# A decoder layer on one core: single rows' maxima, sums and a copy moved behind the prompt's join and copy, memory keys turned behind shares, roots written in place

## The chip, the cores and the metric

The kernel runs on one core of one Trainium2 chip. The metric is the device time of one execution in microseconds (us), lower is better. The core's engines run side by side, each through its own list of instructions in order: TensorE (PE, with PEld for its weight loads), VectorE (DVE), ScalarE (ACT), GpSimd (POOL) and SyncE (SP), which issues most transfers. Semaphores tie the lists together.

## What is computed

One layer of a hybrid decoder for a prompt of 512 rows and a sample group of 8 sequences of 4 rows, with the same weights (model width 1024, float32). Each sub-layer is normalised before and after (RMS norm) and added to the residual:

```python
# 1. mixer: one input projection, split into mLSTM heads and differential-attention heads
p = softmax(mask(q @ k.T) * 64 ** -0.5)       # two components a head, 4 heads
a = p[:, :, 0] - lam * p[:, :, 1]             # the "join"
o = a @ v                                     # then a norm of each head, a gain, w_out
# sample rows: the same, over 256 cached keys read through a page table, and 4 new ones
# 2. memory attention: q = w_mq(norm(x)), 4 heads of 256 over 256 memory tokens,
#    prompt: keys and values from mem_prompt; sample: cache_mem_k, cache_mem_v of each sequence
# 3. ConvFFN: up projection, causal depthwise conv of width 3, SiLU gate, down projection
def rms_norm(x, g):
    return x * lax.rsqrt(jnp.mean(x * x, axis=-1, keepdims=True) + 1e-6) * g
```

## The kernel before

Rows are tiled by 128: four prompt tiles and one of 32 sample rows. Projections run at full precision from two parts of a number each: a weight stage `wst` of 512 KB is loaded by SP, ACT casts its high part (L146) and DVE subtracts to get the low part (L147), together a slot `wslot`. The pool of slots holds four; `Weights` keeps a plan of slots and emits the next as one comes free (`plan`, `pump`, `free`); a slot in the set `extra` comes from another pool, called through `S`, and is emitted without taking one of the four. TensorE then does three matmuls a block: high by high (L411), high by low (L412) and low by high (L413), or the like in L472 and L485.

The order of instructions on each engine is set by a scheduler that goes through the program in the order in which it is written, with a model of each engine's time; `tc.issue_after(x)` holds the instructions written under it until after x. The differential attention goes in steps of one prompt tile and head, sixteen in all, through a software pipe: `da_soft` (two score products `sda`, negated maxima `nm` L1260 on DVE, two exponentials `pda` with sums `su` L1261 on ACT, the reciprocal L1263, L1264 and the join `pda` L1265 on DVE), two turns later `da_turn` (transposes `tpa` L1273 on PE, copied to `aT` L1275 on ACT), then `da_av` (`oda` L1285) and, after every fourth step, `da_end`, which calls `da_post` (square `dasq` L1099 on ACT, sums `dass` L1101 on DVE, root `dars` L304 and product L1103 on POOL, transposes `dat` L1106 on PE, `dtm` L1108 on DVE).

Between the prompt's steps go those of the sample's sequences, in pairs: keys `tpk` are turned on PE (L1229) and copied to `kT` (L1230, one half of them on ACT, one on DVE), scores `ssc` (L1242), a mask added on DVE (L1245), then `sample_exp` (negated maximum `snm` L1052 on DVE, exponential `das` L1053 on ACT). When all eight are done, `sample_softmax` weighs them into one block (`spa` L1072), copies that on ACT to `spc` (L1074), takes two prompt steps (`between`, which is `step` at the call), and turns the copy (`spt` L1085).

In the memory attention `ch_soft` is a prompt step (scores `sca` L1455, maxima `cnm` L1459, exponentials `cp` L1462, reciprocal `csu` L1463, shares `cp` L1465 on DVE) and `ch_turn` turns the shares on PE (`cpt` L1474) and splits them to `pT`; `ch_out` multiplies by the values (`cpo` L1486). Each sequence's keys are 1024 wide in two tiles; `mk_turn` turns one sequence's on DVE by two block transposes of 128x1024 in place (`kvt` or `wst`, L1508), `mk_scores` makes `ssc` (L1528). `ql` (L1439) is the low part of the queries, made on DVE from `w_mq`'s product.

`rstd` writes the root of a mean square into a small tile `rs` on POOL (L302, L304). After it a copy on DVE put it where it is used: in `mrs` at the start (L540, twice) and in `rsd` (L1178, five times, at each projection's end that is followed by a norm); `rsd` is spread over partitions by PE (`rsb` L1737), and the normalised rows are turned (`tp` L332), scaled to `ht` (L334) and split into `fT` (L146 on ACT, L147 on POOL). The last prompt tile's end (L1953 to L1956) adds the residual in three pieces, columns 0 to 511 and 768 to 1023 on DVE and 512 to 767 on POOL, and stores each from SP.

Of the kernel before, what the change touches and what calls it, by code (L numbers as in the profile page):

```python
# [12 lines left out]
ALU = mybir.AluOpType  # L13
# [64 lines left out]
def kernel(ctx: ExitStack, tc: tile.TileContext, I, O):  # L78
# [145 lines left out]

    def slotA(w, k0, n0, nrow=256, share=False):
        def emit():
            st, s = v2(stage(), 512), slot_tile()
            sv = s.rearrange("p l (k n) -> p l k n", k=2)
# [11 lines left out]

    def slotsA(w, n0, share=False):
        for k in range(0, 8, 2):
            slotA(w, k, n0, share=share)

# [52 lines left out]

    def rstd(ss, n, w, dim, name="rs"):

        r = small(w, name)  # L300
        if dim is not None:
            nc.gpsimd.tensor_scalar(out=r[:n], in0=ss, scalar1=1.0 / dim, scalar2=EPS, op0=MUL, op1=ADD)  # L302
            ss = r[:n]
        GTT(out=r[:n], in0=ss, in1=mhalf[:n, :w], op=ALU.pow)  # L304
        return r[:n]

# [232 lines left out]
    for b in range(2):  # L539
        VCP(out=mrs[:, b:b + 1], in_=rstd(sumsq(xms[b], P, N("hN")), P, 1, DM))  # L540
    W.nslots = NSLOT
# [513 lines left out]
    def sample_softmax(sall, su, coef, sel, oname, between=None):  # L1055
# [14 lines left out]
        for e in range(2):  # L1070
            for i in range(NB // 2):
                mm(pa[NS * i:NS * i + NS, :w], lhsT=csz[:, 2 * i + e, :], rhs=sall[:, 2 * i + e, :], start=(e == 0), stop=(e == 1))  # L1072
        a = Z("spc")[:, :w]
        nc.scalar.copy(out=a, in_=pa[:, :w])  # L1074
        behind = between() if between else None
        return a, attend_T(a, oname, behind)
# [19 lines left out]
    def da_post(o, n, c0):  # L1096
# [3 lines left out]
        ss = small(4, "dass")[:n]  # L1100
        VRED(out=ss, in_=sq, axis=AX.X, op=ADD)  # L1101
        rs = rstd(ss, n, 4, P, "dars")
# [16 lines left out]
    def proj_add(xt, gname, src, gname2, dst, order=None, scale=None):  # L1119
# [52 lines left out]
        def rows_of(x, n, c0):  # L1172
            if scale is None:
                pend.append((norm_rows(x, n, ACTROWS), n, gname2, target[0], c0, POOLQ))
                return
            pend.append((x, n, gname2, target[0], c0, POOLQ))
            rs = sm.tile([P, 1], F32, name="rsd", tag="rsd", bufs=5)
            VCP(out=rs[:n], in_=rstd(sumsq(x, n, Z("sqx").bitcast(BF16)[:n]), n, 1, DM))  # L1178
            scale[1].append((rs[:n], c0, n))
# [34 lines left out]

    kst, kts, pts, aTs, outs, rcs = {}, {}, {}, {}, {}, {}

# [15 lines left out]
    def dk_scores(b):  # L1232
# [11 lines left out]
        for c, ps in pair.items():  # L1244
            VTT(out=ps[:, 256:260], in0=ps[:, 256:260], in1=con("cm4"), op=ADD)  # L1245
            sample_exp(sall, c, ps, nm, su)

    def da_soft(i):
# [15 lines left out]
        VTS(out=rc[:, 1:2], in0=rc[:, 1:2], scalar1=su[:, 0:1], scalar2=nlam, op0=MUL, op1=MUL)  # L1264
        STT(out=pt[:, 0, :nk], in0=pt[:, 1, :nk], scalar=rc[:, 1:2], in1=pt[:, 0, :nk], op0=MUL, op1=ADD)  # L1265
        rcs[i] = rc

    def da_turn(i):
# [5 lines left out]
        aTs[i] = Z("aT")  # L1274
        nc.scalar.copy(out=aTs[i][:, :nk], in_=tp[:, :nk])  # L1275

# [30 lines left out]
    def step():  # L1307

        next(prompt)
        next(prompt)  # L1310
        return summed[0].ins

# [51 lines left out]
    for n0 in (0, 512):  # L1364
        slotsA(w_out, n0)
    for n0 in (0, 512):
# [77 lines left out]

    pTs, cps, scored = {}, {}, [None]

    def ch_soft(i):
# [16 lines left out]
        for j in range(2):  # L1464
            VTS(out=p[:, j, :], in0=p[:, j, :], scalar1=su[:, j:j + 1], scalar2=None, op0=MUL)  # L1465

# [165 lines left out]
    for b in range(0, NB, 2):  # L1632
# [3 lines left out]
        if b < 6:  # L1636
            if b:
                mk_turn(b + 2)
            mk_turn(b + 3)
            if b:  # L1640
# [212 lines left out]
    for gi, js in enumerate(groups):  # L1853
# [87 lines left out]
        def end(b):  # L1941
# [3 lines left out]
            if b == TORD[-1]:  # L1945
# [3 lines left out]
                for o, w in ((512, 256), (0, 512), (768, 256)):  # L1949
# [4 lines left out]
                    else:  # L1954
                        STT(out=xb[:, c], in0=z, scalar=rs, in1=xb[:, c], op0=MUL, op1=ADD)
                    dma(out=out[:, c], in_=xb[:, c])  # L1956
                return
# [105 lines left out]
```

## Time and profile before

| what | value |
| --- | --- |
| median of 3 runs | 934.09 us (933.4 to 935.85) |
| the profiled execution's own time | 933.45 us |
| its span | 931.7 us |
| TensorE's granted clock over the span | 0.996 |
| PE busy | 913.5 us (98%) |
| DVE busy | 606.5 us (65%) |
| ACT busy | 377.7 us (41%) |
| POOL busy | 223.0 us (24%) |
| HBM read and written | 112.54 MB and 16.93 MB, 139 GB/s over the span |

Busy time counts instructions with work, not waits or the issue of transfers. In a row of the timeline stand the start, the duration of the group (of several, if a count stands behind x), engine, line, operation and tiles; a bracket gives the idle time of that engine just before, and what ended it. Steps and sequences are named here by their number from zero, in the order of the program: tpa 5 is the transpose of the prompt's step 5.

### The profile page before, as it was taken

How to read it: one execution, taken by the hardware profiler on the slowest of the kernel's cores; microseconds unless marked ns; L12 is line 12 of the kernel's file. 1: busy time of each engine (PE TensorE's matmuls, PEld its weight loads, DVE VectorE, ACT ScalarE, POOL GpSimd, SP SyncE). 2: the span in 40 equal slices, each digit the busy share in tenths (PEclk: the TensorE clock that was granted, in tenths of full speed). 3: DMA queues.
4: the chain of work that ended last, by engine and by line, in shares of the span. 5: the costliest groups of instructions: out<-in, count | busy, mean ns of one | idle time of the engine just before them, and what ended most of it. 6: DMA issues, size and time to landing. Idle time of an engine off the chain costs nothing. (4 is left out here: it accounts for less than half of the span.)

```text
span 931.7 us, 17473 instructions
## 1 busy us (share of the span) xinstructions
PE 913.5 (98%) x6780; PEld 797.6 (86%) x6780; DVE 606.5 (65%) x1128; ACT 377.7 (41%) x728; POOL 223.0 (24%) x475
## 2 busy tenths in 40 slices
PE   9999999999999999999999999999999999999995
PEld 6899787879866778998877899899888998999974
DVE  5845144565888338768645878547748775776767
ACT  5745233344587437724534533322212221222232
POOL 6611000034442126581000642001001110110114
PEclk9999999999999999999999999999999999999998
DMA  9960023335780439966777631152044304412023
GB/s 284 313 192 4 1 91 139 91 102 164 237 294 19 136 107 293 300 214 236 293 244 194 200 108 53 38 168 69 27 137 137 91 4 131 122 47 91 25 94 118
DMA packets 120834, 130.59 MB, mean 140 GB/s; under 512 B 8599, under 2 KB 86264, under 8 KB 120752
## 3 DMA queue, kind: packets, MB, share of 16 engines
q1 hardware_dynamic: 114568, 125.96, 42.9%
q10 hardware_dynamic: 6184, 3.53, 1.2%
q8 instruction: 53, 0.87, 0.4%
q14 instruction: 29, 0.24, 0.1%
HBM read 112.54 MB, written 16.93 MB: 139 GB/s over the span
## 5 line engine op out<-in xcount | busy, mean ns | idle before, releaser
L485 PE MATMUL mm<-fT,wslot 128*128 128x256 f32 x1872 | 235.9, 288 | 0.0
L485 PEld LDWEIGHTS mm<-fT,wslot 128*128 128x128 f32 x1872 | 234.4, 188 | 1.8 <-issue 0.8
L146 ACT CAST wslot<-wst 128x1024 fp32r<-128x1024 f32 x125 | 130.4, 1049 | 255.0 <-issue 72.5
L147 DVE TENSOR_TENSOR wslot<-wst,wslot 128x1024 fp32r<-128x1024 f32 x125 | 154.2, 1239 | 76.1 <-ACT wslot L146 75.7
L1869 PE MATMUL mm<-wslot,act 128*128 128x512 f32 (+1 forms) x180 | 69.3, 387 | 0.0
L1872 PE MATMUL mm<-wslot,act 128*128 128x512 f32 (+1 forms) x172 | 67.1, 391 | 0.0
L1873 PE MATMUL mm<-wslot,act 128*128 128x512 f32 (+1 forms) x172 | 66.8, 392 | 0.0
L1771 POOL COPY cvo<-u 128x2 f32<-128x2 f32 x43 | 10.4, 242 | 217.4 <-DVE u L1769 217.4
L411 PE MATMUL mm<-wslot,hT 128*128 128x512 f32 x128 | 51.3, 402 | 0.0
L413 PE MATMUL mm<-wslot,hT 128*128 128x512 f32 x128 | 51.0, 399 | 0.0
L485 PE MATMUL mm<-hT,wslot 128*128 128x256 f32 (+1 forms) x384 | 50.9, 289 | 0.0
L412 PE MATMUL mm<-wslot,hT 128*128 128x512 f32 x128 | 50.8, 397 | 0.0
L1766 DVE TENSOR_TENSOR u<-mm,rsb 128x256 f32<-128x256 f32 x43 | 18.1, 424 | 48.4 <-PE mm L485 48.4
L485 PEld LDWEIGHTS mm<-hT,wslot 128*128 128x128 f32 x384 | 49.2, 188 | 0.5 <-issue 0.2
L1869 PEld LDWEIGHTS mm<-wslot,act 128*128 128x128 f32 x180 | 34.3, 191 | 8.0 <-issue 0.4
L1873 PEld LDWEIGHTS mm<-wslot,act 128*128 128x128 f32 x172 | 32.3, 188 | 6.9 <-issue 0.4
L1872 PEld LDWEIGHTS mm<-wslot,act 128*128 128x128 f32 x172 | 32.3, 188 | 6.9
L1783 ACT ACTIVATE c<-c 128x560 f32<-128x560 f32 x21 | 14.1, 672 | 57.2 <-DVE c L1777 57.1
L1777 DVE SCALAR_TENSOR_TENSOR c<-u,cvT,c 128x560 f32<-128x560 f32 x43 | 34.4, 799 | 0.9
L1776 DVE SCALAR_TENSOR_TENSOR c<-u,cvT,c 128x560 f32<-128x560 f32 x43 | 34.1, 794 | 0.2
L1884 DVE TENSOR_TENSOR yp<-mm,yp 128x512 f32<-128x512 f32 (+1 forms) x41 | 27.1, 673 | 4.5 <-PE mm L1873 4.3
L413 PEld LDWEIGHTS mm<-wslot,hT 128*128 128x128 f32 x128 | 24.1, 188 | 5.0
(497 smaller groups left out, 1857.5 us busy)
## 6 DMA issues: line engine op xcount, KB each, us to landing
wst<-in_w_up_dram SPq DMA_DIRECT2D x42, 512.0 KB
wst<-in_w_in_dram SPq DMA_DIRECT2D x28, 512.0 KB
wst<-in_w_down_dram SPq DMA_DIRECT2D x20, 512.0 KB
kvt<-in_cache_mem_k_dram SPq DMA_DIRECT2D x10, 512.0 KB
kvt<-in_cache_mem_v_dram SPq DMA_DIRECT2D x10, 512.0 KB
wst<-in_w_mk_dram SPq DMA_DIRECT2D x8, 512.0 KB
xb<-in_x_prompt_dram SPq DMA_DIRECT2D x8, 512.0 KB
wst<-in_cache_dk_dram SPq DMA_DIRECT2D x16, 256.0 KB
```

Source lines behind the costliest of these rows:

```text
L146: nc.scalar.copy(out=hi, in_=src)
L147: (eng or nc.vector).tensor_tensor(out=lo, in0=src, in1=f32(hi), op=SUB)
L411: mm(ps[b], lhsT=xt.hi(k, c0, c0 + n), rhs=s[:, 0, kk, :], start=(k == 0), stop=False)
L412: mm(ps[b], lhsT=xt.hi(k, c0, c0 + n), rhs=s[:, 1, kk, :], start=False, stop=False)
L413: return mm(ps[b], lhsT=xt.lo(k, c0, c0 + n), rhs=s[:, 0, kk, :], start=False, stop=(k == nk - 1))
L485: mm(ps[i], lhsT=s[:, l, k, :], rhs=x(k, c0, c1), start=(k == 0 and j == 0), stop=(k == 7 and j == 2))
L1776: STT(out=c, in0=u[:, 1:EXT - 1], scalar=w[1], in1=c, op0=MUL, op1=ADD)
L1777: STT(out=c, in0=u[:, 0:EXT - 2], scalar=w[0], in1=c, op0=MUL, op1=ADD)
L1869: mm(ps, lhsT=t[:, 0, c0:c0 + P], rhs=s[:, 0, i % 2, cs], start=st, stop=False)
L1872: mm(ps, lhsT=t[:, 0, c0:c0 + P], rhs=s[:, 1, i % 2, cs], start=False, stop=False)
L1873: return mm(ps, lhsT=t[:, 1, c0:c0 + P], rhs=s[:, 0, i % 2, cs], start=False, stop=en)
L1884: VTT(out=y, in0=ps, in1=y, op=ADD)
```

## The change

Seven edits. `rstd` can write its root straight to its place, and the seven copies (L540, L1178) go. `sample_softmax` calls `between` before it copies spa to spc, and that copy is issued after the copy to aT of the first of the two prompt steps. The sums `dass` are issued after the join of a later prompt step (5, 9, 13 or 15). The mask's addition to the sample's scores of an odd sequence b and its neighbour is issued after the join of prompt step b. The first slot of the second half of `w_out` is an extra one. For sequences under 6 the transposes of the memory keys are issued after shares of prompt step b // 2 + 1. The last piece of the last tile is stored from ACT's queue.

```diff
@@ -222,9 +222,12 @@
 
-    def slotA(w, k0, n0, nrow=256, share=False):
+    def slotA(w, k0, n0, nrow=256, share=False, extra=False):
+        if extra:
+            W.extra.add(len(W.plan))
+
         def emit():
-            st, s = v2(stage(), 512), slot_tile()
+            st, s = v2(stage(), 512), S([P, 2, 1024], F32R, "wslot") if extra else slot_tile()
             sv = s.rearrange("p l (k n) -> p l k n", k=2)
...
             if nrow == 256:

@@ -238,9 +241,9 @@
 
-    def slotsA(w, n0, share=False):
+    def slotsA(w, n0, share=False, extra=False):
         for k in range(0, 8, 2):
-            slotA(w, k, n0, share=share)
+            slotA(w, k, n0, share=share, extra=extra and k == 0)
 
...
         if extra:

@@ -295,14 +298,15 @@
 
-    def rstd(ss, n, w, dim, name="rs"):
-
-        r = small(w, name)
+    def rstd(ss, n, w, dim, name="rs", out=None):
+
+        r = small(w, name) if dim is not None or out is None else None
         if dim is not None:
...
             ss = r[:n]
-        GTT(out=r[:n], in0=ss, in1=mhalf[:n, :w], op=ALU.pow)
-        return r[:n]
+        out = r[:n] if out is None else out
+        GTT(out=out, in0=ss, in1=mhalf[:n, :w], op=ALU.pow)
+        return out
 
...
         ss = small(1, name)

@@ -537,7 +541,7 @@
     for b in range(2):
-        VCP(out=mrs[:, b:b + 1], in_=rstd(sumsq(xms[b], P, N("hN")), P, 1, DM))
+        rstd(sumsq(xms[b], P, N("hN")), P, 1, DM, out=mrs[:, b:b + 1])
     W.nslots = NSLOT
...
     def mem_k():

@@ -1070,9 +1074,10 @@
                 mm(pa[NS * i:NS * i + NS, :w], lhsT=csz[:, 2 * i + e, :], rhs=sall[:, 2 * i + e, :], start=(e == 0), stop=(e == 1))
+        behind, first = between() if between else (None, None)
         a = Z("spc")[:, :w]
-        nc.scalar.copy(out=a, in_=pa[:, :w])
-        behind = between() if between else None
+        with tc.issue_after(first) if between else nullcontext():
+            nc.scalar.copy(out=a, in_=pa[:, :w])
         return a, attend_T(a, oname, behind)
...
     def attend_T(a, oname, behind=None):

@@ -1098,7 +1103,8 @@
         ss = small(4, "dass")[:n]
-        VRED(out=ss, in_=sq, axis=AX.X, op=ADD)
+        with tc.issue_after(joined[min(c0 // P * H + 5, 4 * H - 1)].ins):
+            VRED(out=ss, in_=sq, axis=AX.X, op=ADD)
         rs = rstd(ss, n, 4, P, "dars")
...
         pv = v2(at("dat"), P)[:, :, :n]

@@ -1175,7 +1181,7 @@
             rs = sm.tile([P, 1], F32, name="rsd", tag="rsd", bufs=5)
-            VCP(out=rs[:n], in_=rstd(sumsq(x, n, Z("sqx").bitcast(BF16)[:n]), n, 1, DM))
+            rstd(sumsq(x, n, Z("sqx").bitcast(BF16)[:n]), n, 1, DM, out=rs[:n])
             scale[1].append((rs[:n], c0, n))
...
         def mid():

@@ -1212,7 +1218,7 @@
 
-    kst, kts, pts, aTs, outs, rcs = {}, {}, {}, {}, {}, {}
+    kst, kts, pts, aTs, outs, rcs, joined, copied = {}, {}, {}, {}, {}, {}, {}, {}
 
...
         st = stage()

@@ -1242,7 +1248,8 @@
         for c, ps in pair.items():
-            VTT(out=ps[:, 256:260], in0=ps[:, 256:260], in1=con("cm4"), op=ADD)
+            with tc.issue_after(joined[b].ins):
+                VTT(out=ps[:, 256:260], in0=ps[:, 256:260], in1=con("cm4"), op=ADD)
             sample_exp(sall, c, ps, nm, su)
...
     def da_soft(i):

@@ -1262,7 +1269,7 @@
         VTS(out=rc[:, 1:2], in0=rc[:, 1:2], scalar1=su[:, 0:1], scalar2=nlam, op0=MUL, op1=MUL)
-        STT(out=pt[:, 0, :nk], in0=pt[:, 1, :nk], scalar=rc[:, 1:2], in1=pt[:, 0, :nk], op0=MUL, op1=ADD)
+        joined[i] = STT(out=pt[:, 0, :nk], in0=pt[:, 1, :nk], scalar=rc[:, 1:2], in1=pt[:, 0, :nk], op0=MUL, op1=ADD)
         rcs[i] = rc
...
     def da_turn(i):

@@ -1272,7 +1279,7 @@
         aTs[i] = Z("aT")
-        nc.scalar.copy(out=aTs[i][:, :nk], in_=tp[:, :nk])
+        copied[i] = nc.scalar.copy(out=aTs[i][:, :nk], in_=tp[:, :nk])
 
...
 

@@ -1307,8 +1314,9 @@
         next(prompt)
+        first = copied[max(copied)].ins
         next(prompt)
-        return summed[0].ins
+        return summed[0].ins, first
 
...
     F.run(4)

@@ -1362,7 +1370,7 @@
     for n0 in (0, 512):
-        slotsA(w_out, n0)
+        slotsA(w_out, n0, extra=n0 > 0)
     for n0 in (0, 512):
...
     for m in range(8):

@@ -1442,7 +1450,7 @@
 
-    pTs, cps, scored = {}, {}, [None]
+    pTs, cps, scored, shares = {}, {}, [None], {}
 
...
         h, bp = i // 2, i % 2

@@ -1462,7 +1470,7 @@
         for j in range(2):
-            VTS(out=p[:, j, :], in0=p[:, j, :], scalar1=su[:, j:j + 1], scalar2=None, op0=MUL)
+            shares[i] = VTS(out=p[:, j, :], in0=p[:, j, :], scalar1=su[:, j:j + 1], scalar2=None, op0=MUL)
 
...
         h, bp = i // 2, i % 2

@@ -1634,9 +1642,10 @@
         if b < 6:
-            if b:
-                mk_turn(b + 2)
-            mk_turn(b + 3)
+            with tc.issue_after(shares[b // 2 + 1].ins):
+                if b:
+                    mk_turn(b + 2)
+                mk_turn(b + 3)
             if b:
...
         if b == 4:

@@ -1953,7 +1962,7 @@
                         STT(out=xb[:, c], in0=z, scalar=rs, in1=xb[:, c], op0=MUL, op1=ADD)
-                    dma(out=out[:, c], in_=xb[:, c])
+                    (nc.scalar.dma_start if o == 768 else dma)(out=out[:, c], in_=xb[:, c])
                 return
...
             rs = rstd(yss[b, 512], n, 1, None)

```

What this does to the order on the engines, in three places. First VectorE around the joins (L1265) of prompt steps 5 and 6 (pda_2964 and pda_3024 before, pda_2962 and pda_3022 now; rc is the reciprocal, ssc the scores of sequences 4 and 5, nm the maxima of step 7; what was line 1265 is now line 1272). Before, from the sums on:

```order
L1101 TENSOR_REDUCE dass_3094<-dasq_3092 128x4
L1245 TENSOR_TENSOR ssc_3041<-ssc_3041,cpk_87 128x4
L1263 RECIPROCAL rc_2977<-su_2966 128x2
L1245 TENSOR_TENSOR ssc_3046<-ssc_3046,cpk_87 128x4
L1052 TENSOR_REDUCE snm_2570<-ssc_3041 128x1
L1264 TENSOR_SCALAR rc_2977<-rc_2977,su_2966,nlam_570 128x1
L1052 TENSOR_REDUCE snm_2570<-ssc_3046 128x1
L1263 RECIPROCAL rc_3037<-su_3026 128x2
L1265 SCALAR_TENSOR_TENSOR pda_2964<-pda_2964,rc_2977 128x256
L1264 TENSOR_SCALAR rc_3037<-rc_3037,su_3026,nlam_570 128x1
L1265 SCALAR_TENSOR_TENSOR pda_3024<-pda_3024,rc_3037 128x256
```

The sums, the additions and the maxima snm all stood ahead of the first join. Now, from the join of step 5 on:

```order
L1272 SCALAR_TENSOR_TENSOR pda_2962<-pda_2962,rc_2975 128x256
L1252 TENSOR_TENSOR ssc_3039<-ssc_3039,cpk_87 128x4
L1252 TENSOR_TENSOR ssc_3044<-ssc_3044,cpk_87 128x4
L1107 TENSOR_REDUCE dass_3092<-dasq_3090 128x4
L1270 RECIPROCAL rc_3035<-su_3024 128x2
L1056 TENSOR_REDUCE snm_2568<-ssc_3039 128x1
L1056 TENSOR_REDUCE snm_2568<-ssc_3044 128x1
L1271 TENSOR_SCALAR rc_3035<-rc_3035,su_3024,nlam_568 128x1
L1267 TENSOR_REDUCE nm_3120<-sda_3122 128x1
L1267 TENSOR_REDUCE nm_3120<-sda_3123 128x1
L1272 SCALAR_TENSOR_TENSOR pda_3022<-pda_3022,rc_3035 128x256
```

They now stand behind the join of step 5, and together with the maxima of step 7 ahead of the join of step 6.

TensorE at the same place: oda and tpa are those of the prompt's steps, dat the turned rows of the first prompt tile, tpk and kT keys of sequences 6 and 7. Before:

```order
L1106 MATMUL dat_3100<-cpk_87,dasq_3092 128x128 x4
L1229 MATMUL tpk_3140<-cpk_87,wst_3071 128x128 x4
L1229 MATMUL tpk_3146<-cpk_87,wst_3071 128x128 x4
L1285 MATMUL oda_3152<-dvN_1305,aT_3119 128x128 x2
L1273 MATMUL tpa_3156<-cpk_87,pda_3024 128x128 x2
L1257 MATMUL sda_3164<-dkT_1303,dqT_1304 128x384
L1258 LDWEIGHTS cb_114
L1258 MATMUL sda_3164<-cb_114 128x128
L1257 MATMUL sda_3165<-dkT_1303,dqz_2557 128x384
L1258 LDWEIGHTS cb_114
L1258 MATMUL sda_3165<-cb_114 128x128
L1242 MATMUL ssc_3178<-kT_3138,qz_2553 32x260 x4
```

dat and both tpk lay between the scores of step 7 and oda, with oda, tpa and the scores of step 8 between them and the ssc that reads kT. Now, from tpa on:

```order
L1280 MATMUL tpa_3154<-cpk_87,pda_3022 128x128 x2
L1264 MATMUL sda_3162<-dkT_1301,dqT_1302 128x384
L1265 LDWEIGHTS cb_114
L1265 MATMUL sda_3162<-cb_114 128x128
L1264 MATMUL sda_3163<-dkT_1301,dqz_2555 128x384
L1265 LDWEIGHTS cb_114
L1265 MATMUL sda_3163<-cb_114 128x128
L1112 MATMUL dat_3098<-cpk_87,dasq_3090 128x128 x4
L1235 MATMUL tpk_3138<-cpk_87,wst_3069 128x128 x4
L1235 MATMUL tpk_3144<-cpk_87,wst_3069 128x128 x4
L1248 MATMUL ssc_3176<-kT_3136,qz_2551 32x260 x4
L1248 MATMUL ssc_3181<-kT_3055,qz_2551 32x260 x4
```

They now stand behind the scores of step 8, directly ahead of that ssc; between the scores of step 7 and tpa of step 6 only oda is left.

VectorE in the memory attention, from the maxima of step 1 on (cnm_5065 before, cnm_5063 now; kvt are the keys of sequences, two transposes each; cp shares). Before:

```order
L1459 TENSOR_REDUCE cnm_5065<-sca_5052 128x2
L1508 STREAM_TRANSPOSE kvt_5122<-kvt_5122 128x1024
L1463 RECIPROCAL csu_5066<-csu_5066 128x2
L1508 STREAM_TRANSPOSE kvt_5122<-kvt_5122 128x1024
L1465 TENSOR_SCALAR cp_5068<-cp_5068,csu_5066 128x256 x2
L1439 SCALAR_TENSOR_TENSOR ql_4806<-mm_5026,qh_4807 128x256
L1439 SCALAR_TENSOR_TENSOR ql_4806<-mm_5027,qh_4807 128x256
L147 TENSOR_TENSOR pT_5126<-cpt_5129,pT_5125 128x256
L1459 TENSOR_REDUCE cnm_5151<-sca_5138 128x2
L1508 STREAM_TRANSPOSE kvt_5119<-kvt_5119 128x1024
L147 TENSOR_TENSOR pT_5128<-cpt_5129,pT_5127 128x256
L1508 STREAM_TRANSPOSE kvt_5119<-kvt_5119 128x1024
```

Two transposes stood ahead of the first shares in this piece and two more behind them. Now:

```order
L1467 TENSOR_REDUCE cnm_5063<-sca_5050 128x2
L1471 RECIPROCAL csu_5064<-csu_5064 128x2
L1473 TENSOR_SCALAR cp_5066<-cp_5066,csu_5064 128x256 x2
L1516 STREAM_TRANSPOSE kvt_4863<-kvt_4863 128x1024 x2
L1447 SCALAR_TENSOR_TENSOR ql_4804<-mm_5024,qh_4805 128x256
L1447 SCALAR_TENSOR_TENSOR ql_4804<-mm_5025,qh_4805 128x256
L1467 TENSOR_REDUCE cnm_5149<-sca_5136 128x2
L147 TENSOR_TENSOR pT_5124<-cpt_5127,pT_5123 128x256
L1471 RECIPROCAL csu_5150<-csu_5150 128x2
L1473 TENSOR_SCALAR cp_5152<-cp_5152,csu_5150 128x256 x2
L147 TENSOR_TENSOR pT_5124<-cpt_5193,pT_5123 128x256
L1516 STREAM_TRANSPOSE kvt_4939<-kvt_4939 128x1024 x2
```

No transposes of kvt stand ahead of the shares any more; the first two (kvt_4863) follow directly behind them. Further on, behind the shares of step 3, stand four in a row:

```order
L1516 STREAM_TRANSPOSE kvt_5021<-kvt_5021 128x1024
L147 TENSOR_TENSOR pT_5126<-cpt_5193,pT_5125 128x256
L1471 RECIPROCAL csu_5216<-csu_5216 128x2
L1473 TENSOR_SCALAR cp_5218<-cp_5218,csu_5216 128x256 x2
L1516 STREAM_TRANSPOSE kvt_5117<-kvt_5117 128x1024 x2
L1516 STREAM_TRANSPOSE kvt_5120<-kvt_5120 128x1024 x2
```

Before, no transpose of keys was left behind the shares of step 3.

## The prediction

> **What bounds the kernel now.** I read the shares of the span first, then the busy time by stretches, then the waits of TensorE, and last the timelines around each of those waits. Shares and stretches (stretch: length, busy time and count of PE, PEld, DVE, ACT, POOL, then granted clock, DMA share, GB/s):
>
> ```profile
> PE 913.5 (98%) x6780; PEld 797.6 (86%) x6780; DVE 606.5 (65%) x1128; ACT 377.7 (41%) x728; POOL 223.0 (24%) x475
> ...
> 240.00:290.00 50.00, 46.85 (x415) 34.76 (x413) 42.78 (x124) 38.05 (x123) 16.48 (x21) 1.00 0.72 240
> 340.00:425.00 85.00, 85.00 (x562) 78.19 (x562) 61.06 (x80) 46.55 (x84) 49.52 (x107) 1.00 0.77 247
> 425.00:460.00 35.00, 34.28 (x557) 30.16 (x556) 27.59 (x64) 19.26 (x68) 3.86 (x11) 1.00 0.84 322
> 535.00:550.00 15.00, 14.71 (x117) 14.52 (x116) 9.73 (x21) 3.50 (x6) 8.17 (x17) 1.00 0.36 120
> 920.00:931.70 11.70, 0.23 (x2) 0.02 (x1) 6.67 (x13) 2.20 (x8) 3.12 (x4) 0.71 0.32 118
> ```
>
> TensorE is the bound: 913.5 of 931.7 us. Of the 18.2 us in which it stands still, 11.47 lie in the tail after the last matmul; 3.15 lie in the differential attention, 0.72 in the memory attention and 0.29 at the first feed-forward weights (each the stretch less PE's busy time). No other engine's busy time matters, only which of its results TensorE waits for. Those waits by name (engine, operation, line <- what it waited for: total, times, longest):
>
> ```profile
> PE tpa L1273 <- DVE pda L1265: 1.4, 2, 1.1
> PE oda L1285 <- ACT aT L1275: 0.9, 1, 0.9
> PE cpt L1474 <- DVE cp L1465: 0.7, 1, 0.7
> PE mm L412 <- DVE wslot L147: 0.3, 1, 0.3
> PE mm L472 <- ACT fT L146: 0.3, 1, 0.3
> ```
>
> The edits touch all five. So the question is not whether these waits go, but what each reordered engine is late for next. I sum it stage by stage.
>
> **The maxima, sums and copy of the differential attention.** Start, duration, engine, line, operation; in square brackets the idle time before it and its releaser:
>
> ```profile
> 264.69 0.71 PE L1285 MATMUL oda<-dvN,aT 128*128 128x128 f32 x4
> 266.46 0.41 PE L1273 MATMUL tpa<-cpk,pda 128*128 128x128 f32 x2 [1.05 <-DVE pda L1265]
> 267.74 0.61 PE L1106 MATMUL dat<-cpk,dasq 128*128 128x128 f32 x4
> 268.18 1.04 PE L1229 MATMUL tpk<-cpk,wst 128*128 128x128 f32 x8
> 269.05 0.61 PE L1285 MATMUL oda<-dvN,aT 128*128 128x128 f32 x4
> 271.27 1.08 PE L1242 MATMUL ssc<-kT,qz 128*32 128x260 f32 x16
> 278.86 0.94 PE L1285 MATMUL oda<-dvN,aT 128*128 128x128 f32 x6 [0.88 <-ACT aT L1275]
> ```
>
> ```profile
> 264.13 0.68 DVE L1101 TENSOR_REDUCE dass<-dasq 128x4 f32<-128x512 f32 x1
> 265.44 0.42 DVE L1052 TENSOR_REDUCE snm<-ssc 128x1 f32<-128x260 f32 x1
> 265.85 0.47 DVE L1265 SCALAR_TENSOR_TENSOR pda<-pda,rc 128x256 f32<-128x256 f32 x1
> 266.53 1.06 DVE L1265 SCALAR_TENSOR_TENSOR pda<-pda,rc 128x256 f32<-128x256 f32 x1
> 267.52 0.84 DVE L1260 TENSOR_REDUCE nm<-sda 128x1 f32<-128x256 f32 x2
> 269.36 0.67 DVE L1230 COPY kT<-tpk 128x512 f32<-128x512 f32 x1
> ```
>
> ```profile
> 266.28 1.04 POOL L1103 TENSOR_TENSOR dasq<-dao,dars 128x512 f32<-128x512 f32 x1
> ```
>
> The 1.05 us before the first transposes (tpa) is the join of step 5 standing behind one sum (0.68) and two maxima (0.42 each). All three now stand behind that join, so it can run from about 264.95 to 265.4, where TensorE is free at 265.4. I take 0.9 of the 1.05 as gained. But dass, both mask adds, both maxima and the pair nm of step 7 now stand ahead of the join of step 6: 0.68 + 0.14 + 0.8 + 0.84 and the reciprocals, which puts that join at about 267.9, ending at 268.35 with the usual 0.47, or 268.95 with the 1.06 that it has now. TensorE reaches its transposes earlier than before, at about 267.45, because in its new order only four oda matmuls stand between the scores of step 7 and tpa of step 6; dat and tpk (268.18 − 267.74 + 269.05 − 268.18 = 1.31 us of work) have moved behind. A new gap of 0.9 to 1.5, taken as 1.2.
>
> The 1.06 of that join is itself a lead: it is more than double its twin's 0.47, and POOL multiplies dasq from 266.28 to 267.32 beside it. The Trainium skill, "SBUF — State Buffer", section "Who interferes with whom", with the section before it on the two sides, says that a VectorE instruction with two SBUF inputs and a GpSimd instruction that reads SBUF take one port pair in turn, and the second is held until the first is done. This trace's pair of rows agrees; by that rule the gap would be the upper value and the sum 0.3 more.
>
> Since tpk now ends directly before ssc 6 and 7, whose keys are copied out of tpk by VectorE in 0.67, a second new gap stands there: 0.6 to 1.0, taken as 0.7 + 0.2 for the semaphores, 0.9. Before, oda, tpa and two sda pairs lay between. The 0.88 at 278.86 (spc copied ahead of aT on ACT) goes wholly, since spc now follows the next aT and its reader spt has moved behind two more steps. Stage: −0.9 + 1.2 + 0.9 − 0.9 = +0.3. Bounds: −1.9 if neither new gap shows, +1.2 with both at the upper value.
>
> **The fifth slot for the second half of w_out.** Before, its first slot waits for a free slot:
>
> ```profile
> 339.72 0.50 PE L412 MATMUL mm<-wslot,mixT 128*128 128x512 f32 x1 [0.29 <-DVE wslot L147]
> ```
>
> With one slot split in the differential attention, the rest are split one slot earlier, and this wait goes. The three matmuls ahead take 0.87 instead of the 0.70 that three of 0.23 spacing take, so up to 0.46 is to be had; I take 0.4. Its price is one more cast (about 1.05 us on ACT) and subtraction (about 1.24 on DVE) at 273 to 275, behind the maxima of ssc 7 and ahead of nm of step 9. In the stretch 240 to 290 VectorE works 42.78 of 50, so this cover is thin: if nm of step 9 comes late, 0 to 1.2 more is paid there. I take 0, since oda and tpa of earlier steps stand on TensorE between those scores and their use, and keep 1.2 as a bound.
>
> **Weight loads ahead of row loads.** That slot moves the w_mv and w_mq loads one place earlier on SP, ahead of mem_d's and x rows' transfers; in 340 to 425 TensorE now stands still for 0.00 us at a DMA share of 0.77. A gain is excluded, there being no wait. A row that lands late is bounded by the waits for a weight here, 0.29 and, for two in a row with the xb load behind them, about 1. I take +0.2.
>
> **The transposes of the memory keys.**
>
> ```profile
> 430.25 0.65 DVE L1459 TENSOR_REDUCE cnm<-sca 128x2 f32<-128x512 f32 x1
> 430.82 1.23 DVE L1508 STREAM_TRANSPOSE kvt<-kvt 128x1024 f32<-128x1024 f32 x1
> 431.99 0.17 DVE L1463 RECIPROCAL csu<-csu 128x2 f32<-128x2 f32 x1
> 432.07 1.22 DVE L1508 STREAM_TRANSPOSE kvt<-kvt 128x1024 f32<-128x1024 f32 x1
> 433.21 0.63 DVE L1465 TENSOR_SCALAR cp<-cp,csu 128x256 f32<-128x256 f32 x2
> ```
>
> ```profile
> 433.71 0.74 PE L1474 MATMUL cpt<-cpk,cp 128*128 128x128 f32 x4 [0.67 <-DVE cp L1465]
> 438.69 3.34 PE L1486 MATMUL cpo<-pT,mvN 128*128 128x512 f32 x12
> 442.40 1.97 PE L1528 MATMUL ssc<-kvt,qx 128*32 128x128 f32 x64
> ```
>
> The shares of step 1 stand behind two transposes of 1.2; without them they end near 430.4, and the 0.67 goes: −0.7. But all ten halves of kvt now follow shares: one tile (two halves) those of step 1, a tile and a half those of step 2, and from the rest of the third tile on, two whole tiles in a row, those of step 3. Adding the rows up from 428.0 (cnm 0.6, 1.15 from cnm's end to csu, shares 0.55, a transpose 1.17, ql pair 0.66, pT 0.33) the second key tile is turned at about 438.55 and the fifth at 447.55. TensorE, 0.7 earlier, comes to ssc 12 at 438.0, since this now stands ahead of cpo: a gap of 0.55. From there cpo in part (6 at 0.27), cpt, sca, the rest of ssc 12 and 13 and cpo bring it to ssc 15 at about 445.9: a gap of up to 1.65. Taken in full, since no filler lies between: −0.7 + 0.55 + 1.65 = +1.5. Bounds: −0.8 if the transposes come in time, +2.5 if another tile slips by one more transpose.
>
> **Roots written in place.**
>
> ```profile
> 539.01 0.16 DVE L1178 COPY rsd<-rs 128x1 f32<-128x1 f32 x1 [0.95 <-POOL rs L304]
> 539.08 1.28 DVE L334 TENSOR_TENSOR ht<-tp,gT 128x512 f32<-128x512 f32 x2
> 540.47 2.78 PE L472 MATMUL mm<-fT,wslot 128*128 128x288 f32 x19 [0.29 <-ACT fT L146]
> ```
>
> This one copy holds VectorE 0.95 us for POOL; behind it wait two ht, the casts to fT on ACT, and TensorE. Without it ht starts at about 538.1 and the 0.29 goes, 0.45 start to start: −0.45 (bounds −0.5 and 0, the latter if POOL's subtraction for fT, not the cast, is then last). The other six copies, 0.15 each, stand where TensorE shows no wait: 0.
>
> **The last store from ACT's queue.**
>
> ```profile
> 926.66 1.61 DVE L1955 SCALAR_TENSOR_TENSOR xf<-zy,rs,xf 128x512 f32<-128x512 f32 x2 [0.73 <-POOL rs L304]
> 927.43 1.69 SPq L1956 DMA_DIRECT2D out_dram<-xf  x3
> ```
>
> The three stores are issued one after another until 929.12, though the last piece is done at 928.27. On another queue the third can go at about 928.3 rather than after the second: −0.35, between 0 and −0.45 (1.69/3 = 0.56 per issue at most). The rule that speaks against more is in the Trainium skill, "DMA: Bandwidth & Descriptors", section "Issuing engines are not separate DMA queues": the same 16 DMA engines carry the bytes, and only the issue time is saved. No run here shows that yet.
>
> **Sum.** +0.3 − 0.4 + 0.2 + 1.5 − 0.45 − 0.35 = +0.8 us. The profiled execution took 933.45 us (span 931.7 and 1.75 around it), so 934.25 there. It is 0.64 under the median of the three runs, 934.09; on the median's footing 934.9. Less than 0.3% (2.8 us) either way can't be told from no change.
>
> **Rivals.** *Faster: no new gap.* All of today's waits go and nothing is late: 1.05 + 0.88 in the differential attention, 0.7 in the memory attention, 0.46, 0.45 and 0.35: −3.9, 930.2. For it: every removed wait has its row. Against: it needs the transposes of the fifth tile 1.65 us sooner than the rows add up to, and dat and tpk no longer fill. It decides where the new gaps together stay under 1.1.
>
> *Slower: VectorE's backlog of turned keys.* In the memory attention VectorE carries five tiles of 2.34 us each behind shares; if the chain share, pT, next maximum also slips by the four transposes in a row (4.7), cpt 4 and 5 and the scores behind them wait too: +2.5 in the stage instead of +1.5 by the bound above, and 1.5 more where cpo next waits for pT: 0.8 + 1.0 + 1.5 = +3.3, 937.4; it decides from 2 us more than I summed. For it: the DVE rows above stand back to back. Against: over the stretch 425 to 460 VectorE works 27.59 of 35, which leaves 7.4 to catch up in.
>
> *The gaps are only passed on.* Each removed wait returns at the next instruction that needs the same late result, and all engines meet again at the stage's end: 0 in both attentions, −1.0 from the rest, 933.1. This is "the same" too.
>
> **Chances and range.** Forecast with its new gaps 0.45, waits passed on 0.22, faster rival 0.16, slower rival 0.17. The first has a spread of some 2 us either way by the bounds above, and so spills about 0.03 to the slower side. Faster by over 0.3%: 0.17; within: 0.63; slower: 0.20. Range 930.6 to 937.2: it reaches into the faster rival's spread and just short of the slower one's value.
>
> **What would show it.** Right: no idle before tpa of step 5, cpt of step 1, the first fT matmul and the L412 matmul; new idle before tpa of step 6 (DVE pda), ssc 6 (DVE kT), ssc 12 and 15 (DVE kvt); the third store issued beside the second. Wrong: stretch 425 to 460 losing under 0.5 us of TensorE time, or the new gaps missing in 260 to 280 (then it is faster); or new waits for weights between 340 and 425 (then the loads' order was mispriced).

## The result and the profile after

The changed kernel takes 938.99 us (median of five runs, 938.07 to 941.36) against 934.09 (933.4 to 935.85): ratio 1.0056, 95% interval 1.0038 to 1.0073. It is slower by about 4.9 us, where 934.9 and no change that can be told were forecast. Its profiled execution took 939.8 us with a span of 938.0, 6.3 more than before.

The stretches of the changed kernel, with the columns of before:

```profile
240.00:290.00 50.00, 46.44 (x383) 34.58 (x386) 42.59 (x125) 36.65 (x122) 17.26 (x23) 1.00 0.74 244
340.00:425.00 85.00, 82.07 (x514) 74.28 (x513) 56.36 (x75) 47.40 (x82) 41.25 (x97) 0.98 0.72 233
425.00:460.00 35.00, 33.99 (x570) 31.28 (x569) 26.51 (x52) 15.66 (x56) 6.29 (x22) 1.00 0.77 290
535.00:550.00 15.00, 15.00 (x128) 15.00 (x127) 11.77 (x20) 5.86 (x11) 11.29 (x19) 1.00 0.66 212
```

And the five longest waits of TensorE between 240 and 470 us (total, times, longest):

```profile
PE mm L476 <- ACT hqT L146: 1.6, 2, 1.3
PE tp L336 <- ACT hN L320: 1.4, 1, 1.4
PE tpa L1280 <- DVE rc L1270: 1.2, 1, 1.2
PE ssc L1536 <- issue: 1.0, 2, 0.6
PE ssc L1248 <- DVE rc L1270: 0.9, 1, 0.9
```

Of the waits that the edits were to remove, those before oda, cpt, L412 and fT are gone and the longest before tpa is down to 0.3. Two shorter ones before tpk (0.5 and 0.3), which the prediction doesn't price, stand as before. Two new ones stand in the differential attention, where the prediction put them. The surprise is the stretch 340 to 425: TensorE stood still for 0.00 us there, and now for 2.93, at a lower granted clock.

Idle time alone doesn't say how much later the work is, so here is the start of the same matmuls in both traces, as the difference after minus before (first or last of a kind, in the order of the program):

| matmul, its start before | difference, us | added in this stretch |
| --- | --- | --- |
| first sda, 243.69 | +1.07 | +1.07 |
| last dat of the prompt, 331.49 | +1.90 | +0.83 |
| last mm of w_mv, 377.25 | +1.34 | −0.56 |
| first sca, 417.97 | +6.77 | +5.43 |
| first mm of the memory's output projection, 473.13 | +6.71 | −0.06 |
| first down-projection mm, 589.28 | +6.34 | −0.37 |
| last down-projection mm, 919.95 | +6.35 | +0.01 |

The first 1.07 can't be put down to an edit: in the profiles of the kernels below this number lies anywhere between −0.29 and +0.94, and at +0.81 and +0.91 in two that have no edit ahead of that place. Most of the rest is one stretch, the queries' projection w_mq, with +5.43.

### The profile page after: what moved, and what is told of

It is laid out like the page before. It is cut to its first block, busy times and chain, and to the rows that moved or that the text cites. A ratio compares the mean times of both kernels' runs of the same rounds, so it can differ in the third digit from the quotient of the medians.

```text
span 938.0 us, 17460 instructions
## 1 busy us (share of the span) xinstructions
PE 914.3 (97%) x6780; PEld 798.8 (85%) x6780; DVE 606.8 (65%) x1121; ACT 377.9 (40%) x728; POOL 216.8 (23%) x475
## 4 chain that ended last, share of the span: by engine, by line
PE 86%; DMA 5%; DVE 4%; ACT 3%; issue 1%; POOL 0%; ACTq 0%; DVEq 0%; SPq 0%; POOLq 0%
PE mm L489 33%; PE mm L415 7%; PE mm L416 7%; PE mm L417 7%; PE mm L476 6%; PE mm L1878 3%; PE mm L1882 3%; PE mm L1881 3%; PE mm L394 2%; PE sda L1264 2%; PE cpo L1494 1%; PE sca L1463 1%; PE oda L1292 1%; PE ssc L1536 1%; PE tp L336 1%
```

## The experiments

The kernel before was run again beside each group, so its median differs a little between them (934.22 to 934.34). Where an edit of the change is made alone, the diff is against the kernel before, shortened to its decisive lines.

**Without the extra slot.** The first theory (A) was that the slot puts loads in a worse order.

```diff
-        slotsA(w_out, n0, extra=n0 > 0)
+        slotsA(w_out, n0)
```

> The changed kernel without the extra slot for w_out; the other six edits stay, and the order of the loads between 340 and 390 us is again that of before. Theory A (the extra slot moves two w_mq loads and an x load ahead of mk_d's; ScalarE then waits for mk_d with the norm behind it, TensorE stands still for 2.9 us at 380 to 397 and the clock is cut for some us behind that: +5.4 there, less 0.5 at w_out): 934.1 (939.0 less 4.9), no wait of TensorE for hN or hqT. Theory B (the reordered joins and key transposes cost most of it, as summed ahead of the run): 937 to 938, waits for hN or hqT still there or their cost returned elsewhere.

Measured: 935.47 us (before 934.34), ratio 1.0007 (0.9998 to 1.0016). No wait for hN or hqT, and the stretch of w_mq is at +0.00. It is 1.4 us above the 934.1 of theory A. The other six edits together cost nothing that is clear of noise (0.7 us by the ratio); theory B falls.

**The extra slot alone.**

```diff
-        slotsA(w_out, n0)
+        slotsA(w_out, n0, extra=n0 > 0)
```

> The kernel before with the extra slot alone. Theory A: 934.1 + 4.9 = 939.0, with the L412 wait at 339.7 gone, a wait of TensorE for hN of about 1.4 and for hqT of about 1.3 at 380 us, and a granted clock of about 0.5 in the two us behind them. Theory B: 933.6 to 934.5. If the clock is cut in some runs alone: about 937 and a wide spread.

Measured: 939.84 us, ratio 1.0053 (1.0039 to 1.0067). The L412 wait is gone, with −0.57 up to the end of w_mv, and +5.25 follows in w_mq, behind three waits of TensorE:

```profile
378.92 1.09 PE L335 MATMUL tp<-cpk,hN 128*128 128x128 f32 x8 [1.23 <-ACT hN L319]
381.32 9.88 PE L475 MATMUL mm<-hqT,wslot 128*128 128x256 f32 x81 [1.31 <-ACT hqT L146]
395.44 13.02 PE L475 MATMUL mm<-hqT,wslot 128*128 128x288 f32 x96 [1.55 <-ACT hqT L146]
```

The granted clock is 1.00 there, where about 0.5 was expected. So the slot alone is enough, and the fall of the clock in the changed kernel's trace is not needed for it.

What it does is seen on VectorE in the additions of rows (xb, in the order sample, tiles 0 to 3) and the last tile of the first half (y). Before; then with the slot alone:

```profile
340.98 0.68 DVE L1138 TENSOR_TENSOR y<-mm,gb 128x512 f32<-128x512 f32 x1
345.16 1.40 DVE L1166 SCALAR_TENSOR_TENSOR xb<-y,rs,xb 32x512 f32<-32x512 f32 x2 [0.66 <-POOL rs L304]
...
358.38 1.40 DVE L1166 SCALAR_TENSOR_TENSOR xb<-y,rs,xb 128x512 f32<-128x512 f32 x2
...
367.06 3.48 DVE L1166 SCALAR_TENSOR_TENSOR xb<-y,rs,xb 128x512 f32<-128x512 f32 x2
...
377.65 1.40 DVE L1166 SCALAR_TENSOR_TENSOR xb<-y,rs,xb 128x512 f32<-128x512 f32 x2
```

```profile
344.41 0.68 DVE L1141 TENSOR_TENSOR y<-mm,gb 128x512 f32<-128x512 f32 x1
348.71 1.40 DVE L1169 SCALAR_TENSOR_TENSOR xb<-y,rs,xb 32x512 f32<-32x512 f32 x2
...
362.93 0.75 DVE L1169 SCALAR_TENSOR_TENSOR xb<-y,rs,xb 128x512 f32<-128x512 f32 x1 [1.85 <-DMA xb<-in_x_prompt_dram]
...
365.18 0.74 DVE L1169 SCALAR_TENSOR_TENSOR xb<-y,rs,xb 128x512 f32<-128x512 f32 x1
...
372.63 1.42 DVE L1169 SCALAR_TENSOR_TENSOR xb<-y,rs,xb 128x512 f32<-128x512 f32 x2 [2.65 <-POOL hqT L147]
384.35 2.44 DVE L1169 SCALAR_TENSOR_TENSOR xb<-y,rs,xb 128x512 f32<-128x512 f32 x2
```

The first half's last tile is finished 3.4 us later, because the scheduler, with three slots of the second half ready instead of two, puts their matmuls on TensorE ahead of that tile's last two slots: 48 of them stand ahead of its last slot in the order of the program, instead of 36. The sample's rows are behind that tile on VectorE, and behind them hangs a chain: addition, store, load of the next x tile, next addition. Each x tile has a buffer of its own. What ties the links is SP's list, where the load stands directly behind the store, and the store waits for its addition:

```profile
365.94 0.34 SPq L1170 DMA_DIRECT2D x_d<-xb  x1
366.39 0.37 SPq L1148 DMA_DIRECT2D xb<-in_x_prompt_dram  x1
```

The chain starts 3.5 late and ends 6.7 late (384.35 against 377.65); of this about 0.6 stands already at the last dat. The addition at 372.63 is put down to POOL's hqT, which it does not read; its rows are those of the load issued at 366.39, which had landed at 372.56. Then the norm, hN, the turn and hqT follow, and TensorE has nothing else: its first two waits follow the addition at 372.63 (367.06 before), the third the one at 384.35. That last one had its rows by 380.46 and stood behind VectorE's low parts of a slot and of mk_d.

My first reading, that ScalarE stands behind mk_d's load, holds for a small part only:

```profile
373.83 1.06 ACT L146 CAST mkT<-wst 128x1024 fp32r<-128x1024 f32 x1 [2.56 <-DMA wst<-mk_d]
374.79 1.05 ACT L312 ACTIVATE hN<-xb 128x1024 f32<-128x1024 f32 x1
```

The norm's first pass starts behind the cast of mk_d, at 374.79, where the row addition ended at 374.05, so the cast holds the norm by 0.74 us.

**The slot, with the matmuls held.** This was to tell the late chain (A1) from the order of the loads (A2). The diff comes on top of the line of the slot.

```diff
-                    one(b, k, slots[k // 2])
+                    with tc.issue_after(hold) if hold is not None and b < 4 and k == 4 else nullcontext():
+                        t = one(b, k, slots[k // 2])
+                    if b < 4:
+                        last[0] = t.ins
...
-            run(gemmA(xt, 8, [4, 0, 1, 2, 3], ev1, block_major=True, before=before, mid=mid, midk=1 if scale else MIDK))
+            run(gemmA(xt, 8, [4, 0, 1, 2, 3], ev1, block_major=True, before=before, mid=mid, midk=1 if scale else MIDK, hold=None if scale else last[0]))
```

> The kernel before with the extra slot alone, and with the third and fourth slot of w_out's second half held back on TensorE until the first half's last tile is done (as they stood before). Theory A1 (the slot costs because TensorE now takes those slots first, so that the first half's last tile, the first store of rows and each x load behind it come some 3.5 us later, and meet the w_mq loads): the first xb addition is back at about 345 us, no wait for hN or hqT, the L412 wait mostly gone: 933.8 to 934.4. Theory A2 (the order of the loads itself: three w_mq loads still go ahead of the third x load and of mk_d's): still 937 or more, with ScalarE waiting for mk_d at about 372.

Measured: 935.17 us, ratio 1.0012 (1.0003 to 1.0021): all but 1.0 of the 5.5 us is back, and the stretch of w_mq is at +0.27, though three w_mq loads still go ahead of the third x load (two before, four with the slot alone).

```profile
341.66 0.68 DVE L1146 TENSOR_TENSOR y<-mm,gb 128x512 f32<-128x512 f32 x1
...
346.87 1.40 DVE L1174 SCALAR_TENSOR_TENSOR xb<-y,rs,xb 32x512 f32<-32x512 f32 x2
...
379.66 1.40 DVE L1174 SCALAR_TENSOR_TENSOR xb<-y,rs,xb 128x512 f32<-128x512 f32 x2
```

The chain starts 1.7 late instead of 3.5 and ends 2.0 late instead of 6.7; the slot's own gain is gone too (+0.30 up to the end of w_mv instead of −0.57). So the cost comes from the matmuls that go ahead, as A1 has it, though the first addition is not back at 345 and the time is 0.8 above the upper end expected. The order at the third x load costs at most the 1.0 that is left. What is not separated is the late start from the loads that a late chain meets: with the slot alone a w_mv load (352.86) and a w_mq load (354.86) go ahead of the second x load (356.57), whose addition waits 1.85 for its rows; held, as before the change, neither does, and that addition does not wait. Putting the x loads ahead of the stores on SP's list would try this; no run here does.

**Roots alone.**

```diff
-        VCP(out=mrs[:, b:b + 1], in_=rstd(sumsq(xms[b], P, N("hN")), P, 1, DM))
+        rstd(sumsq(xms[b], P, N("hN")), P, 1, DM, out=mrs[:, b:b + 1])
...
-            VCP(out=rs[:n], in_=rstd(sumsq(x, n, Z("sqx").bitcast(BF16)[:n]), n, 1, DM))
+            rstd(sumsq(x, n, Z("sqx").bitcast(BF16)[:n]), n, 1, DM, out=rs[:n])
```

> The kernel before with the roots written in place alone (seven copies away, no other order changes). Theory C (this edit is what shifted the start of the changed kernel by 1.06 us up to 55 us, through the two mrs copies): start shifted by +1.0, -0.4 at the fT matmul: 934.7. Rival: the shift at the start is a difference from run to run or from another edit: 933.7.

Measured: 934.03 us against 934.34, ratio 0.9995 (0.9986 to 1.0004); the fT wait is gone, −0.25 in its stretch. This profile starts +0.65 late, and that alone would not speak against theory C; but the profiles of the key transposes alone and of the maxima alone, which have the copies still, start +0.91 and +0.81 late. So C isn't needed, and the start stays unexplained. The gain itself is plain: the stretch down to 589 is at −0.25 to −0.37 in the four kernels with the roots in place, and at −0.08 to +0.34 in the others.

**The three attention edits, and each by itself.**

```diff
-        nc.scalar.copy(out=a, in_=pa[:, :w])
+        with tc.issue_after(first) if between else nullcontext():
+            nc.scalar.copy(out=a, in_=pa[:, :w])
...
-        VRED(out=ss, in_=sq, axis=AX.X, op=ADD)
+        with tc.issue_after(joined[min(c0 // P * H + 5, 4 * H - 1)].ins):
+            VRED(out=ss, in_=sq, axis=AX.X, op=ADD)
...
-            VTT(out=ps[:, 256:260], in0=ps[:, 256:260], in1=con("cm4"), op=ADD)
+            with tc.issue_after(joined[b].ins):
+                VTT(out=ps[:, 256:260], in0=ps[:, 256:260], in1=con("cm4"), op=ADD)
```

> The kernel before with the three edits of the differential attention alone (sums, mask additions and maxima behind joins, the copy spc behind aT). From the changed kernel's trace (shift from 253 to 331 us: +0.83): 934.9, with new waits before the transposes of step 6 (about 1.2) and before ssc 6 (about 0.9), and none before step 5's and oda 8. If the waits are only passed on to each other: 934.1.

Measured: 936.3 us, ratio 1.0022 (1.0013 to 1.0032): 2.0 us, 1.1 more than the changed kernel's trace gave. In its trace the stage adds +1.55, with the new waits at 1.18 and 0.87.

The copy alone (the first of these three edits):

> The kernel before with the copy spc behind aT alone. If the 0.88 before oda 8 goes and nothing comes for it: 933.4. If spt, moved behind, or the two prompt steps ahead of it pass it on: 934.3.

Measured: 934.55 us, ratio 1.0003 (0.9994 to 1.0012). The 0.88 before oda 8 goes, and a wait of 0.76 for an aT comes at 315.55, 37 us later. That one stands in the four profiles that have this edit and not the slot (0.46 to 0.76), and neither in the changed kernel nor in a kernel without this edit. That the wait is passed on to it is the likely reading, and not shown further.

The sums and the mask additions (the second and third):

> The kernel before with sums and mask additions (and so the maxima) behind the joins alone. From the run with all three edits of the stage (+2.0) less what the copy gives there (0.9 if it stands by itself): 937.2, with the waits before tpa 6 (1.2) and ssc 6 (0.9); if the copy gives nothing by itself: 936.3.

Measured: 936.67 us, ratio 1.0023 (1.0014 to 1.0032). The sums with the maxima carry the whole cost.

The sums only (the second):

> The kernel before with the sums dass alone behind the joins; mask additions and maxima stay ahead. This edit alone moves dat and tpk on TensorE behind the scores of step 8. If that move is the cost (no filler ahead of tpa 6, no cover ahead of ssc 6): about 936. If it is the maxima between the joins: 934.3.

Measured: 935.78 us, ratio 1.0016 (1.0007 to 1.0025), with the wait of 0.88 before ssc 6, 0.54 before tpa 5 and none before tpa 6. So dass alone makes most of it. The wait before ssc 6 goes with the move of dat and tpk: here they stand behind the scores of step 8, and in the next run, where they don't, there is none. The 1.18 before tpa 6 appears only where sums and maxima are both moved.

The mask additions, and with them the maxima, only (the third):

> The kernel before with the mask additions (and so the maxima) alone behind the joins; dass stays ahead, dat and tpk stay where they were. If the maxima between the joins are the cost: about 936. If the move of dat and tpk is: the join of step 5 comes 0.8 earlier, dat and tpk fill, 933.6.

Measured: 934.18 us, ratio 1.0003 (0.9994 to 1.0012): no cost, and of the gain hoped for no sign in the time either, though the wait before tpa 5 falls from 1.05 to 0.45.

**GpSimd's product beside the join.** To see whether the product stretches the join, it was to follow it:

```diff
-        GTT(out=sq, in0=o, in1=rs.unsqueeze(2).broadcast_to([n, H, P]), op=MUL)
+        with tc.issue_after(joined[min(c0 // P * H + 6, 4 * H - 1)].ins):
+            GTT(out=sq, in0=o, in1=rs.unsqueeze(2).broadcast_to([n, H, P]), op=MUL)
```

> The run with sums and mask additions alone (936.7), and the product dasq on GpSimd held behind the join of step 6 as well. Theory P (the join of step 6 took 1.30 instead of 0.47 because GpSimd read its operands at the same time): the join takes 0.47 to 0.50, the wait before tpa 6 falls from 1.18 to about 0.35, total 935.9. Rival (the join is slow for its own operands): still 1.30 and 1.18, total 936.7 or more.

Measured: 936.27 us, ratio 1.0023 (1.0013 to 1.0034), and nothing learned from it directly: the edit leaves the list of every engine as it was, and the product started at 268.61 and the join at 268.63, together as before. So this is the kernel with the sums and the mask additions measured a second time, and it tells something else: the stretch 418 to 473 is at +0.73 in this profile and at −0.09 in the other, so what differs there comes from the execution. The other runs shift the join and the product against each other by themselves. The join of step 6 and the product, in the run with the three attention edits, the one with the maxima alone, and the one with the sums alone:

```profile
267.47 1.30 DVE L1268 SCALAR_TENSOR_TENSOR pda<-pda,rc 128x256 f32<-128x256 f32 x1
```

```profile
267.46 1.04 POOL L1105 TENSOR_TENSOR dasq<-dao,dars 128x512 f32<-128x512 f32 x1
```

```profile
267.49 0.92 DVE L1266 SCALAR_TENSOR_TENSOR pda<-pda,rc 128x256 f32<-128x256 f32 x1
```

```profile
267.09 1.04 POOL L1103 TENSOR_TENSOR dasq<-dao,dars 128x512 f32<-128x512 f32 x1
```

```profile
267.67 0.47 DVE L1266 SCALAR_TENSOR_TENSOR pda<-pda,rc 128x256 f32<-128x256 f32 x1
```

```profile
268.32 1.04 POOL L1104 TENSOR_TENSOR dasq<-dao,dars 128x512 f32<-128x512 f32 x1
```

In the first two the join ends 0.27 and 0.28 behind the product's end (268.77 and 268.50, 268.41 and 268.13), wherever it began; in the third it takes its 0.47 where it is done before the product begins. Before the change it was 0.27 (267.59 and 267.32). That is what the Trainium skill, "SBUF — State Buffer", section "Who interferes with whom", says: the second of the two is held until the first is done. Why the join then ends 0.27 behind, and not its whole 0.47, stays open. It is an agreement of traces, not an experiment that took the product away.

**Key transposes alone.**

```diff
-            if b:
-                mk_turn(b + 2)
-            mk_turn(b + 3)
+            with tc.issue_after(shares[b // 2 + 1].ins):
+                if b:
+                    mk_turn(b + 2)
+                mk_turn(b + 3)
```

> The kernel before with the key transposes behind the shares alone. The sum ahead of the run had +1.5: 935.8. The trace of the changed kernel says that the 0.67 before cpt goes and two waits of some 0.5 before ssc come, none at ssc 14 and 15, whose transposes end before TensorE arrives: +0.2, 934.5.

Measured: 934.37 us, ratio 1.0001 (0.9992 to 1.0010). The wait before cpt is gone, but it is gone too in eight profiles where no key transpose was moved, so that is not shown to be this edit's work. The stretch 418 to 473 has −0.07, where kernels without the edit have −0.29 to +0.73. The two waits before ssc ("issue", 0.76 and 0.23) are no work of this edit: they stand also in the profiles of the slot alone and of the maxima alone (0.72 to 0.75 each), and differ between the two measurements of one kernel above (1.4 in all against 0.3). Their cause stays open.

**Without the slot and the sums.** Roots, copy and keys as above, and the last store together:

```diff
-                    dma(out=out[:, c], in_=xb[:, c])
+                    (nc.scalar.dma_start if o == 768 else dma)(out=out[:, c], in_=xb[:, c])
```

> The kernel before with the four edits that by themselves cost nothing (roots in place, the copy behind aT, key transposes behind shares, the last store from ScalarE's queue), without the extra slot, the sums and the mask additions. If they add up from the single runs (-0.3, +0.2 and 0 within their uncertainty, and about -0.2 at the end): 933.9. If the removed waits help each other: 933.0.

Measured: 933.32 us against 934.23, ratio 0.9992 (0.9983 to 1.0001). The best of these kernels, but not clear of no change.

## Why the prediction was wrong

**The step that failed is "weight loads ahead of row loads",** sized at +0.2 with 1 as its end; +5.43 came in its stretch. The argument went from SP's order alone: which load stands ahead of which. It bounded a late row by the waits that this stretch had already had, 0.29 and about 1, as if a late row could cost no more than they did. What mattered was one list further: the slot that is ready earlier is taken by TensorE ahead of other work, and that work, the first half's last tile, starts a chain of stores and loads with a period of 5.7 to 10.6 us per tile (additions at 345.16, 350.89, 358.38, 367.06 and 377.65 before). The sum counted the −0.4 of the slot and not what its matmuls displace; the slot alone brought +5.25 in this stretch, and with its matmuls held +0.27. The prediction did name 340 to 425 as a place where it could be wrong, but by waits for weights; TensorE waits for rows there (hN and hqT).

That the terms without the slot came out near is luck, by errors that cancel: +1.1 by the medians of that run (+0.7 by the ratio), +1.0 in the sum (0.8 + 0.4 − 0.2).

**The slot's own gain** was right: −0.4 forecast, −0.57 measured with the slot alone, the L412 wait gone.

**Sums, maxima and copy.** Both new waits were right in place and size (1.2 and 0.9 forecast). The changed kernel:

```profile
266.76 0.41 PE L1280 MATMUL tpa<-cpk,pda 128*128 128x128 f32 x2 [0.29 <-DVE ssc L1252]
270.28 0.41 PE L1280 MATMUL tpa<-cpk,pda 128*128 128x128 f32 x2 [1.18 <-DVE rc L1270]
274.35 1.08 PE L1248 MATMUL ssc<-kT,qz 128*32 128x260 f32 x16 [0.88 <-DVE rc L1270]
281.00 0.94 PE L1292 MATMUL oda<-dvN,aT 128*128 128x128 f32 x6
```

The stage was forecast at +0.3; it is +0.83 there and +1.55 with these edits alone. Of the +0.83, 0.41 is TensorE's idle time (3.57 against 3.16), near the forecast; the other 0.4 is put down to nothing here. The copy's 0.9 is gained in the changed kernel, with no later wait for it; by itself the copy gains nothing in the time. The prediction had two lengths for the join ahead of tpa 6, 0.47 and 1.06 beside the product. It took 1.30, and the gap was 1.18 all the same, since TensorE came later too: at 269.10, which is about 268.0 on the footing of before, where I had 267.45.

**Key transposes.** +1.5 forecast, about 0 measured. The gap of 1.65 at ssc 15 did not come. In the run without the slot, whose work is 2.70 later here, VectorE's four transposes in a row are these, and TensorE starts ssc 14 and 15 at 449.63 without a wait:

```profile
444.50 4.62 DVE L1513 STREAM_TRANSPOSE kvt<-kvt 128x1024 f32<-128x1024 f32 x4
```

They end at 449.12, so 446.4 on the footing of before, where I had 447.55; TensorE comes at 446.9, where I had 445.9. Each of the two paths was missed by 1.0 to 1.1 us, in opposite directions, and their difference was the whole term.

**Roots and last store** were near: −0.45 forecast for the roots, −0.37 in the changed kernel. The third store is now issued beside the second:

```profile
934.17 0.91 SPq L1965 DMA_DIRECT2D out_dram<-xf  x2
```

```profile
933.39 1.61 DVE L1964 SCALAR_TENSOR_TENSOR xf<-zy,rs,xf 128x512 f32<-128x512 f32 x2 [0.73 <-POOL rs L308]
```

```profile
935.04 0.34 ACTq L1965 DMA_DIRECT2D out_dram<-xf  x1
```

From the start of the last additions to the end of the span it takes 4.6 us (938.0 − 933.39) against 5.0 (931.7 − 926.66): −0.4, forecast −0.35. In the eleven profiles without this edit it takes 5.0 us, in the three with it 4.6 to 4.8. The gain is less than one issue. In the changed profile the whole tail behind the last matmul is as long as before all the same, since the last additions start 7.1 us behind the last matmul instead of 6.7.

**The rivals.** The slower one was given 0.17 and 937.4, so 3.3 us where 4.9 were measured, but for another cause: VectorE's turned keys, which cost nothing. A right side with a wrong mechanism is no hit.

## What to carry to other kernels

When an edit makes an operand ready earlier, look in the new order for what the work that uses it now stands ahead of, and follow that displaced work down its chain of stores and loads to where TensorE next needs it. A stretch without idle time shows that its chains are in time, not that they have slack; a chain whose links stand behind one another on one queue's list passes each late start on. A wait removed from a bound engine may be worth less than its size, where the next result on the same list is not there yet: the copy's 0.88 went, and its run got no faster.

## What the hardware showed unexpectedly

The granted clock fell within the changed kernel's stall. Two rows of 2 us behind the waits of 1.38 and 1.31 (at 380.36 and 382.76), and the matmuls of that time:

```profile
382.00:384.00 2.00, 1.24 (x6) 1.24 (x7) 2.00 (x3) 2.00 (x5) 1.22 (x1) 0.72 0.22 47
384.00:386.00 2.00, 2.00 (x11) 2.00 (x11) 2.00 (x2) 1.33 (x2) 2.00 (x2) 0.50 0.93 279
```

```profile
382.76 11.28 PE L476 MATMUL mm<-hqT,wslot 128*128 128x256 f32 x81 [1.31 <-ACT hqT L146]
...
396.90 3.31 PE L476 MATMUL mm<-hqT,wslot 128*128 128x288 f32 x23 [0.24 <-ACT hqT L146]
```

That is eleven matmuls in 2 us instead of nineteen or twenty. The 81 matmuls took 11.28 us, and 9.88 with the slot alone, where nearly the same two waits (1.23 and 1.31) left the clock at 1.00. But the third wait is 0.24 here and 1.55 there, and the stretch costs +5.43 here and +5.25 there, so how much of the 5.43 is the clock's can't be told. The Trainium skill, "TensorE: Matmul & The Clock Gate", section "Part 1: The HAM clock gate (the "warmup" mystery)", has the clock fall behind an idle window of about 3.4 us; here no single idle stretch was longer than 1.38 us, and 2.7 us of idleness broken by 1.1 us of transposes was enough in one of two profiles. Here the measurement decides.
